# Two causal convolutions moved from channels in partitions to tokens in partitions, in a two-layer hybrid transformer kernel

## The chip, the cores and the metric

The kernel runs on one core of one Trainium2 chip. The metric is the device time of one execution in microseconds (us). Three runs of the kernel before took 2628.22, 2629.81 and 2631.31 us; their median, 2629.81 us, is the time before.

## What is computed

The reference takes 256 tokens of 2048 features through two layers. Each layer is a normalization, one wide input projection, several mixers on slices of the projection, output projections and a feed-forward part. Two of the mixers are preceded by a causal convolution of width 4 over the tokens, one filter per channel, then `silu`:

```python
def causal_dwconv(u, w, bias):          # layer 1, state space inputs, 1536 channels
    out = lax.conv_general_dilated(u, w[:, None, :], (1,), ((SSD_CONV - 1, 0),), ...)
    return out + bias
xbc = jax.nn.silu(causal_dwconv(xbc, conv_w, conv_b))
xs, bm, cm = _split(xbc, (SSD_WIDTH, N_BC, N_BC))      # 1024 + 256 + 256 channels
...
qkv = jax.nn.silu(causal_depthwise_conv(qkv, conv_w))  # layer 2, delta rule, 3072 channels
q, k, v = jnp.split(qkv, 3, axis=-1)                   # 1024 channels each
...
vb = v * beta[..., None]
```

So a channel's output at token i is `w[3]·u[i] + w[2]·u[i-1] + w[1]·u[i-2] + w[0]·u[i-3]`, plus the bias in layer 1, through `silu(y) = y·sigmoid(y)`. The kernel writes that as `h·(tanh(h) + 1)` with `h = y/2`, which is why its taps and biases are halved. In layer 1 the `xs` part is multiplied by the step sizes and by the skip weights, with tokens in partitions; in layer 2 `v` is multiplied by `beta`, with tokens in partitions too.

## The kernel before

The Tile framework schedules the program: it orders each engine's instructions when the program is built, by readiness in its own model of time and by the order in which they are written, picks the slots of each pool and sets all semaphores. On the chip each engine then runs its own list in that fixed order.

**Panels.** Nearly all of TensorE's work is projections. `panel` computes 256 tokens by up to 512 columns over 16 blocks of the contraction. Every 4 blocks it loads a weight tile `wst` on SP's queue (L201, pool of 3), and for each half of that tile ScalarE makes `whi`, the weights rounded to fp32r (L207, pool of 4), and VectorE makes `wlo`, the rest (L208, pool of 4). Each pair `whi`, `wlo` then feeds 12 matmuls of 512 columns: three products (L192 to L194) for two contraction blocks and two halves of the tokens. All other work of the mixers is laid between these matmuls.

**The convolutions.** `conv_group` (L692) takes the two PSUM tiles of a panel (tokens in partitions, 512 channels). ScalarE scales them into `raw` (L696); TensorE transposes `raw` in eight 128x128 blocks, so that channels lie in partitions (L703); ScalarE multiplies by the last tap (L708 with bias, L710 without); VectorE adds the other three taps with shifted reads along the free dimension, three instructions for each of four channel blocks (L713); then `tanh` (L715) and the product (L716). It is called nine times: for three panels of the state space inputs (L731 to L746: p = 0 and 1 are `xs`, p = 2 is `bm` and `cm`) and for six panels of the delta rule (`gdn_in`, L924: parts k, q, v for two groups of four heads). Where the consumer wants tokens in partitions, `to_tokens` (L719) transposes back, four blocks for each half of the tokens: for `xs` (L741, with ScalarE's copy at L742, then VectorE's products L743 and L744), for the sums of squares of k and q in `gdn_in`, and for `v` in each of the four calls of `gdn_unit` (L990, then the product with `beta` at L991).

**Order around the change.** State space inputs follow the sparse attention of layer 1 and precede the two z panels. In layer 2 the written order is `gdn_in(0)`, `gdn_unit(0, 0)`, `gdn_in(1)`, `gdn_unit(0, 1)`, `gdn_unit(1, 0)`, `gdn_unit(1, 1)`, two more z panels, then the other attention's panels; a unit's long chain of small products runs while panels written later fill TensorE.

**Pools.** `sp` has 7 slots and `s4` 17, of 4 KB per partition each; `s2` has 16 of 2 KB. Before, a convolution holds one `sp` tile (`raw`) and two `s4` tiles (`acc`, `th`). POOL (GpSimd) issues no DMA in this kernel; it computes powers in `rstd` (L159) and clears small tiles (L1004). SP's queue carries the weight tiles; ScalarE's queue carries small loads.

Of the kernel before, what the change touches and what calls it, by code (L numbers as in the profile page):

```python
# [12 lines left out]
AF = mybir.ActivationFunctionType  # L13
# [44 lines left out]
def build(ctx, tc, I, out, tap=None, upto=99):  # L58
# [22 lines left out]
    def s2(shape, dt=F32, name="s2"):  # L81
        return sb.tile(shape, dt, name=name, tag="s2", bufs=N2)
# [4 lines left out]
    def tiny(shape, name, bufs=2):  # L87
        return sm.tile(shape, F32, name=name, bufs=bufs)
# [603 lines left out]
    def conv_group(ps, r, taps, bias):  # L692

        raw = sp([128, 2, 512], name="raw")
        for t in range(2):
            S.activation(raw[:, t], ps[t], AF.Copy, scale=r[:, t:t + 1])  # L696
        acc = s4([128, 4, 256], name="acc")
        for j in range(0, 4, 2):
            pt = psum("tp", [128, 512])
            pv = pt.rearrange("p (k t c) -> p k t c", k=2, t=2)  # L700
            for kk in range(2):
                for t in range(2):
                    PE.transpose(pv[:, kk, t], raw[:, t, (j + kk) * 128:(j + kk + 1) * 128], ident)  # L703
            for kk in range(2):
                c = j + kk
                u = pt[:, kk * 256:(kk + 1) * 256]
                if bias is not None:
                    S.activation(acc[:, c], u, AF.Identity, scale=taps(3, c), bias=bias(c))  # L708
                else:
                    S.activation(acc[:, c], u, AF.Copy, scale=taps(3, c))  # L710
                for k in (2, 1, 0):
                    d = 3 - k
                    V.scalar_tensor_tensor(acc[:, c, d:], u[:, :256 - d], taps(k, c), acc[:, c, d:], op0=OP.mult, op1=OP.add)  # L713
        th = s4([128, 4, 256], name="th")
        S.activation(th, acc, AF.Tanh)  # L715
        V.scalar_tensor_tensor(acc, th, 1.0, acc, op0=OP.add, op1=OP.mult)  # L716
        return acc

    def to_tokens(src, t):  # L719

        ps = psum("tp", [128, 512])
        for c in range(4):
            PE.transpose(ps[:, c * 128:(c + 1) * 128], src[:, c, t * 128:(t + 1) * 128], ident)
        return ps

    def v8(ap):
        return ap.rearrange("p (h d) -> p h d", d=64)

    xsd, xdt = [], []
    BC = None  # L730
    for p in range(3):  # L731
        ps = panel(w_in, 0, 16, 1024 + 512 * p, 512, at_k(xn))
        xc = conv_group(ps, r, lambda j, c: conv_w[:, j * 12 + 4 * p + c:j * 12 + 4 * p + c + 1],
                        lambda c: conv_b[:, 4 * p + c:4 * p + c + 1])
        tap(f"xc{p}", xc)
        if p < 2:
            xsd.append(s4([128, 2, 512], name="xsd"))
            xdt.append(s4([128, 2, 512], name="xdt"))
            for t in range(2):
                pt = to_tokens(xc, t)  # L740
                xs = s2([128, 512], name="xs")  # L741
                S.activation(xs, pt, AF.Copy)  # L742
                V.tensor_tensor(v8(xsd[p][:, t]), v8(xs), b3(d_skip[:, 8 * p:8 * p + 8], 64), op=OP.mult)  # L743
                V.tensor_tensor(v8(xdt[p][:, t]), v8(xs), b3(dts[:, t, 8 * p:8 * p + 8], 64), op=OP.mult)  # L744
        else:
            BC = xc  # L746
# [47 lines left out]
        V.scalar_tensor_tensor(dst, dst, 1.0, ps[t][:, :n], op0=OP.add, op1=OP.mult)  # L794

    yssd = []
    rh = tiny([128, 2], "rh")
    V.tensor_scalar(rh, r, 0.5, None, op0=OP.mult)
    for g in range(2):
        ps = panel(w_in, 0, 16, 512 * g, 512, at_k(xn))  # L800
        ssg = tiny([128, 2], "ssg")
# [122 lines left out]
    def gdn_in(gi):  # L924
        qkv = [None] * 3
        kr, rks, rqs = [], [], []
        for part in (1, 0, 2):
            c0 = 2584 + part * 1024 + gi * 512
            ps = panel(w_in2, 0, 16, c0, 512, at_k(xn))
            if gi == 0 and part == 1:  # L930
                decays()
            ch = part * 8 + gi * 4
            qkv[part] = conv_group(ps, r, lambda j, c: P3[:, j * 24 + ch + c:j * 24 + ch + c + 1], None)
            if part == 2:
                continue
            for t in range(2):
                pt = to_tokens(qkv[part], t)
                sq = s2([128, 4, 128], name="gsq")
                S.activation(flat(sq), pt, AF.Square)
                ss = tiny([128, 4], "sg")  # L940
                V.tensor_reduce(ss, sq, axis=AX.X, op=OP.add)
                if part == 1:
                    kr.append(s2([128, 4, 128], name="kr"))
                    S.activation(flat(kr[t]), pt, AF.Copy)
                    rks.append(rstd(ss, 1.0, f"rk{t}"))
                else:
                    rqs.append(rstd(ss, 1.0, f"rq{t}", 128 ** -0.5))
        GD[gi] = qkv, kr, rks, rqs

    def gdn_unit(gi, t):  # L950
# [33 lines left out]
        for dst, rhs in ((A, lambda i: kbT[:, i]), (W, lambda i: qkv[0][:, i, ts])):  # L984
# [1 line left out]
            for i in range(4):  # L986
                PE.matmul(ps[:, i * 128:(i + 1) * 128], qkv[1][:, i, ts], rhs(i), start=True, stop=True)
            V.tensor_tensor(flat(dst), ps, flat(D), op=OP.mult)
        pt = to_tokens(qkv[2], t)
        vb = s2([128, 4, 128], name="vb")  # L990
        V.tensor_tensor(vb, hd(pt), b3(beta[:, t, hs], 128), op=OP.mult)  # L991

        Tt = s2([128, 4, 128], name="Tt")
        V.tensor_tensor(Tt, A, mid(lv[:, 0:128], 4), op=OP.mult)
# [454 lines left out]
```

## Time and profile before

| | |
|---|---|
| median of three runs | 2629.81 us (2628.22 to 2631.31) |
| the profiled execution | 2627.55 us, of which the span of instructions is 2625.8 us |
| TensorE (PE) busy | 2595.6 us, 99% of the span |
| VectorE (DVE) busy | 2136.2 us, 81% |
| ScalarE (ACT) busy | 1495.5 us, 57% |
| GpSimd (POOL) busy | 43.3 us, 2% |
| DMA | 478.65 MB, mean 182 GB/s |
| granted TensorE clock | 0.997 of full speed over the run |

PE stands for TensorE's matmuls and PEld for its weight loads, which overlap them. A matmul's end is modelled in the profile, so the time that one costs is read from start to start of neighbours and not from its duration. L12 is line 12 of the kernel. "mm" is a panel's PSUM tile, "tp" one for transposes, "sx" one for small products.

### The profile page before, as it was taken

What the parts mean: (1) busy time and instruction counts of PE and PEld (TensorE: products, weight loads), DVE (VectorE), ACT (ScalarE), POOL (GpSimd) and SP (SyncE); (2) the same over time, 40 slices, a digit from 0 to 9 for tenths busy, and PEclk for the clock granted to TensorE, in tenths of its full rate; (3) what the DMA queues carried; (4) which work ended last, traced back from release to release, by engine and by line L of the source; (5) the groups of instructions that cost most, each with busy time, mean ns of one, the idle gap of its engine ahead of it and who ended that gap; (6) DMA issues with size and microseconds to landing.
All of it is one profiled execution on the core that took longest, in us unless ns stands there. A gap on an engine that the chain in (4) does not pass through costs nothing.

```text
span 2625.8 us, 32837 instructions
## 1 busy us (share of the span) xinstructions
PE 2595.6 (99%) x12521; PEld 2164.9 (82%) x12521; DVE 2136.2 (81%) x2970; ACT 1495.5 (57%) x2002; POOL 43.3 (2%) x48
## 2 busy tenths in 40 slices
PE   8999999999999999999999999999999999999998
PEld 8998887888888888888898887888778888888886
DVE  5767789999989999676755867588999999999996
ACT  5455456656657566554533655455667566565663
POOL 0000000000000000000000000000000000000000
PEclk9999999999999999999999999999999999999999
DMA  7454555566655655753432843556455555565554
GB/s 239 143 177 156 169 178 186 183 204 199 196 202 192 194 193 194 227 184 126 132 98 87 263 166 115 178 193 224 170 197 181 206 193 208 192 206 191 196 192 161
DMA packets 181916, 478.65 MB, mean 182 GB/s; under 512 B 9127, under 2 KB 50046, under 8 KB 181758
## 3 DMA queue, kind: packets, MB, share of 16 engines
q1 hardware_dynamic: 175312, 467.05, 53.3%
q10 hardware_dynamic: 6446, 9.51, 1.1%
q8 instruction: 98, 1.61, 0.2%
q14 instruction: 60, 0.49, 0.1%
HBM read 472.32 MB, written 4.21 MB: 181 GB/s over the span
## 4 chain that ended last, share of the span: by engine, by line
PE 88%; DVE 7%; DMA 2%; ACT 2%; issue 1%; ACTq 0%; POOL 0%; POOLq 0%; SPq 0%; DVEq 0%
PE mm L270 24%; PE tp L270 12%; PE sx L270 11%; PE mm L194 10%; PE mm L192 10%; PE mm L193 10%; DVE wlo L282 3%; DMA wst<-in_w_down_dram 1%; ACT whi L281 1%; PE sx L1022 1%; PE sx L1017 1%; PE mm L430 1%; DVE t L303 1%; DMA wst<-in_w_in_dram 1%; PE tp L916 0%
## 5 line engine op out<-in xcount | busy, mean ns | idle before, releaser
L281 ACT ACTIVATE whi<-wst 128x1024 fp32r<-128x1024 f32 (+1 forms) x560 | 543.2, 980 | 312.8 <-PE mm L270 123.7
L282 DVE TENSOR_TENSOR wlo<-wst,whi 128x1024 fp32r<-128x1024 f32 (+1 forms) x560 | 615.8, 1120 | 67.2 <-ACT whi L281 65.1
L208 DVE TENSOR_TENSOR wlo<-wst,whi 128x1024 fp32r<-128x1024 f32 (+6 forms) x336 | 377.4, 1128 | 207.2 <-ACT whi L207 205.6
L207 ACT ACTIVATE whi<-wst 128x1024 fp32r<-128x1024 f32 (+6 forms) x336 | 329.5, 983 | 323.2 <-PE mm L194 290.3
L281 ACT ACTIVATE whi<-t 128x1024 fp32r<-128x1024 f32 x210 | 222.3, 1058 | 260.4 <-DVE t L307 118.7
L282 DVE TENSOR_TENSOR wlo<-t,whi 128x1024 fp32r<-128x1024 f32 x210 | 256.3, 1222 | 49.4 <-ACT whi L281 46.7
L194 PE MATMUL mm<-whi,x2l 128*128 128x512 f32 (+3 forms) x608 | 229.7, 378 | 0.0
L193 PE MATMUL mm<-wlo,x2h 128*128 128x512 f32 (+3 forms) x608 | 228.2, 375 | 1.4 <-DVE wlo L208 1.4
L192 PE MATMUL mm<-whi,x2h 128*128 128x512 f32 (+3 forms) x608 | 228.4, 376 | 0.0
L192 PE MATMUL mm<-whi,xnh 128*128 128x512 f32 (+3 forms) x416 | 152.5, 368 | 2.0 <-ACT whi L207 1.6
L270 PE MATMUL mm<-wlo,xnh 128*128 128x512 f32 x392 | 153.6, 392 | 0.5 <-DVE wlo L282 0.3
L270 PE MATMUL mm<-whi,xnl 128*128 128x512 f32 x392 | 153.1, 390 | 0.0
L270 PE MATMUL mm<-whi,xnh 128*128 128x512 f32 x392 | 151.3, 391 | 1.3 <-ACT whi L281 1.3
L193 PE MATMUL mm<-wlo,xnh 128*128 128x512 f32 (+3 forms) x416 | 151.8, 365 | 0.0
L194 PE MATMUL mm<-whi,xnl 128*128 128x512 f32 (+3 forms) x416 | 150.7, 365 | 0.0
L303 DVE TENSOR_TENSOR t<-wst 128x1024 f32<-128x1024 f32 x105 | 128.2, 1221 | 13.9 <-DMA wst<-in_w_down_dram 10.5
L270 PE MATMUL mm<-wlo,hTh 128*128 128x512 f32 x343 | 134.3, 391 | 0.6 <-DVE wlo L282 0.6
L270 PE MATMUL mm<-whi,hTl 128*128 128x512 f32 x343 | 133.6, 389 | 0.0
L270 PE MATMUL mm<-whi,hTh 128*128 128x512 f32 x343 | 132.1, 391 | 0.0
L193 PEld LDWEIGHTS mm<-wlo,x2h 128*128 128x128 f32 x608 | 114.7, 189 | 17.1 <-DVE wlo L208 2.0
L194 PEld LDWEIGHTS mm<-whi,x2l 128*128 128x128 f32 x608 | 114.5, 188 | 15.4 <-issue 1.0
L192 PEld LDWEIGHTS mm<-whi,x2h 128*128 128x128 f32 x608 | 114.7, 189 | 15.0 <-issue 0.8
(619 smaller groups left out, 5697.2 us busy)
## 6 DMA issues: line engine op xcount, KB each, us to landing
wst<-in_w_up_dram SPq DMA_DIRECT2D x128, 1024.0 KB, 5.1
wst<-in_w_down_dram SPq DMA_DIRECT2D x128, 1024.0 KB, 5.5
wst<-in_w_in_dram SPq DMA_DIRECT2D x84, 1024.0 KB, 5.0
wst<-in_w_out_dram SPq DMA_DIRECT2D x16, 1024.0 KB, 5.5
wst<-in_w_o_dram SPq DMA_DIRECT2D x16, 1024.0 KB, 5.2
wst<-in_w_in_dram SPq DMA_DIRECT2D x16, 780.0 KB, 4.5
wst<-in_w_in_dram SPq DMA_DIRECT2D x12, 824.0 KB, 4.5
wst<-in_w_in_dram SPq DMA_DIRECT2D x12, 736.0 KB, 6.9
```

Of the source, the lines that this page charges most:

```text
L192: PE.matmul(ps[t][:, :n], xh[:, sl], wa, start=kt == first, stop=False)
L193: PE.matmul(ps[t][:, :n], xh[:, sl], wb, start=False, stop=False)
L194: PE.matmul(ps[t][:, :n], xl[:, sl], wa, start=False, stop=kt == last)
L207: S.activation(a[:, :2 * n], src, AF.Copy)
L208: V.tensor_tensor(b[:, :2 * n], src, a[:, :2 * n].bitcast(F32), op=OP.subtract)
L270: PE.matmul(B[b], x, y, start=left[b] == total[b], stop=left[b] == 1)
L281: S.activation(a[:, :n], src, AF.Copy)
L282: V.tensor_tensor(b[:, :n], src, a[:, :n].bitcast(F32), op=OP.subtract)
L303: V.tensor_tensor(t13, s.rearrange("p (k l n) -> p k l n", k=2, l=2)[:, :, 0], s[:, :1024].rearrange("p (l n) -> p l n", l=2)[:, ::-1], op ...
L430: PE.transpose(pv[:, kk, t, :], us[t, l][:, c:c + 128], ident)
L1017: PE.matmul(ps[:, i * 64:(i + 1) * 64].rearrange("p (m b) -> p m b", b=b), N[:, i], half(T[:, i], 0), start=True, stop=True)
L1022: PE.matmul(ps[:, i * 64:(i + 1) * 64].rearrange("p (m b) -> p m b", b=b), P[:, i], half(Tt[:, i], 1), start=True, stop=True)
```

## The change

A new function `conv_tokens` convolves with tokens in partitions. ScalarE scales the panel's PSUM into `raw` (now with half the normalization factor, `rh`, moved up for that). The four taps of the 512 channels come as rows, broadcast to all partitions by two DMAs of 512 KB on SP's queue (`tb`). For each shift d = 1, 2, 3 GpSimd issues two DMAs from SBUF to SBUF: rows 0 to 127-d of both token halves to rows d to 127, and the last d rows of the first half to the first d rows of the second; VectorE clears the first d rows of the first half. VectorE multiplies `raw` and the three shifted copies by their tap rows and adds them up, on tiles of 128x1024. `tanh` and the last product are as before, on the other layout; `th` moves from the `s4` pool to `sp`.

It is used in four of the nine places: p = 0 and 1 of the state space inputs (with a bias row, loaded by a DMA of 256 KB on SP's queue and halved by ScalarE) and part v of both groups of the delta rule. There `raw` isn't transposed, `to_tokens` isn't called, and the copy `xs` falls away; the other five convolutions stay as they were.

```diff
+    def conv_tokens(ps, rh, name, c0, bias=None):
+        w = I[name][0] if len(I[name].shape) == 3 else I[name]
+        wd = w.shape[1]
+        raw = sp([128, 2, 512], name="raw")
+        for t in range(2):
+            S.activation(raw[:, t], ps[t], AF.Copy, scale=rh[:, t:t + 1])
+        tb = [s4([128, 2, 512], name="tb") for _ in range(2)]
+        for q in range(2):
+            nc.sync.dma_start(tb[q], bass.AP(tensor=w.tensor, offset=w.offset + 2 * q * wd + c0,
+                                             ap=[[0, 128], [wd, 2], [1, 512]]))
+        acc = s4([128, 2, 512], name="acc")
+        def row(j):
+            return mid(tb[j // 2][:, j % 2], 2)
+        V.tensor_tensor(acc, raw, row(3), op=OP.mult)
+        if bias is not None:
+            V.tensor_tensor(acc, acc, mid(bias, 2), op=OP.add)
+        for d in (1, 2, 3):
+            sh = sp([128, 2, 512], name="sh")
+            V.memset(sh[:d, 0], 0.0)
+            G.dma_start(sh[d:], raw[:128 - d])
+            G.dma_start(sh[:d, 1], raw[128 - d:, 0])
+            V.tensor_tensor(sh, sh, row(3 - d), op=OP.mult)
+            V.tensor_tensor(acc, acc, sh, op=OP.add)
+        th = sp([128, 2, 512], name="th")
+        S.activation(th, acc, AF.Tanh)
+        V.scalar_tensor_tensor(acc, th, 1.0, acc, op0=OP.add, op1=OP.mult)
+        return acc
...
+    rh = tiny([128, 2], "rh")
+    V.tensor_scalar(rh, r, 0.5, None, op0=OP.mult)
...
-        xc = conv_group(ps, r, lambda j, c: conv_w[:, j * 12 + 4 * p + c:j * 12 + 4 * p + c + 1],
-                        lambda c: conv_b[:, 4 * p + c:4 * p + c + 1])
+        if p < 2:
+            bb = s2([128, 512], name="bb")
+            cb_ = I["conv_b"]
+            nc.sync.dma_start(bb, bass.AP(tensor=cb_.tensor, offset=cb_.offset + 512 * p, ap=[[0, 128], [1, 512]]))
+            S.activation(bb, bb, AF.Copy, scale=0.5)
+            xc = conv_tokens(ps, rh, "conv_w", 512 * p, bb)
+        else:
+            xc = conv_group(ps, r, lambda j, c: conv_w[:, j * 12 + 4 * p + c:j * 12 + 4 * p + c + 1],
+                            lambda c: conv_b[:, 4 * p + c:4 * p + c + 1])
...
-                pt = to_tokens(xc, t)
-                xs = s2([128, 512], name="xs")
-                S.activation(xs, pt, AF.Copy)
+                xs = xc[:, t]
...
+            if part == 2:
+                qkv[part] = conv_tokens(ps, rh, "conv_w_2", ch * 128)
+                continue
...
-        pt = to_tokens(qkv[2], t)
         vb = s2([128, 4, 128], name="vb")
-        V.tensor_tensor(vb, hd(pt), b3(beta[:, t, hs], 128), op=OP.mult)
+        V.tensor_tensor(vb, hd(qkv[2][:, t]), b3(beta[:, t, hs], 128), op=OP.mult)
```

## Rows read from the trace of the kernel before

**Rows 1.** The page: engines (busy us, share of the span, instructions).

```profile
PE 2595.6 (99%) x12521; PEld 2164.9 (82%) x12521; DVE 2136.2 (81%) x2970; ACT 1495.5 (57%) x2002; POOL 43.3 (2%) x48
```

**Rows 2.** The page, chain that ended last: shares of the span by engine.

```profile
PE 88%; DVE 7%; DMA 2%; ACT 2%; issue 1%; ACTq 0%; POOL 0%; POOLq 0%; SPq 0%; DVEq 0%
```

**Rows 3.** Busy time by stretch: length, PE, PEld, DVE, ACT, POOL, clock, DMA share, GB/s.

```profile
206.00:231.00 25.00, 25.00 (x122) 20.66 (x121) 18.91 (x30) 14.78 (x19) 0.00 (x0) 1.00 0.42 130
231.00:255.00 24.00, 24.00 (x115) 19.63 (x114) 18.10 (x26) 13.73 (x17) 0.00 (x0) 1.00 0.55 176
...
1189.00:1213.00 24.00, 24.00 (x126) 20.24 (x126) 21.40 (x37) 12.07 (x17) 0.53 (x1) 1.00 0.48 159
...
1284.00:1308.00 24.00, 24.00 (x164) 23.52 (x162) 22.30 (x42) 13.58 (x22) 0.79 (x2) 1.00 0.41 121
```

**Rows 4.** One line each: transposes there (L703) and back (L723), ns min/median/max.

```profile
L703 PE MATMUL tp<-idt,raw x72: 270/273/328, 208.6 to 1285.1; 128*128 128x128 f32 x72
...
L723 PE MATMUL tp<-idt,acc x64: 270/273/303, 221.7 to 1397.4; 128*128 128x128 f32 x64
```

**Rows 5.** Timeline of PE around the eight transposes back (start, us, instruction).

```profile
221.46 0.39 PE L194 MATMUL mm<-whi,xnl 128*128 128x512 f32 x1
221.69 1.03 PE L723 MATMUL tp<-idt,acc 128*128 128x128 f32 x8
222.48 0.48 PE L192 MATMUL mm<-whi,xnh 128*128 128x512 f32 x1
222.80 0.40 PE L193 MATMUL mm<-wlo,xnh 128*128 128x512 f32 x1
```

**Rows 6.** Timeline of PE around the eight transposes there, p = 1.

```profile
232.13 0.39 PE L192 MATMUL mm<-whi,xnh 128*128 128x512 f32 x1
232.39 0.44 PE L703 MATMUL tp<-idt,raw 128*128 128x128 f32 x2
...
233.14 0.82 PE L703 MATMUL tp<-idt,raw 128*128 128x128 f32 x6
...
234.03 0.40 PE L193 MATMUL mm<-wlo,xnh 128*128 128x512 f32 x1
```

**Rows 7.** Timeline of DVE in the convolution of p = 1.

```profile
235.14 2.42 DVE L713 SCALAR_TENSOR_TENSOR acc<-tp,P2T,acc 128x255 f32<-128x255 f32 x6
237.48 1.22 DVE L208 TENSOR_TENSOR wlo<-wst,whi 128x1024 fp32r<-128x1024 f32 x1
...
243.82 1.22 DVE L716 SCALAR_TENSOR_TENSOR acc<-th,acc 128x1024 f32<-128x1024 f32 x1
```

**Rows 8.** Groups of DVE by form: its two clears (count, busy us, mean ns).

```profile
L1137 DVE MEMSET flu<- 128x64 f32 x4 | 0.4, 112 | 0.0
L1265 DVE MEMSET Pc<- 128x120 f32 x2 | 0.3, 158 | 0.0
```

**Rows 9.** Timeline of ACT: two `whi` of p = 1's panel.

```profile
226.89 1.06 ACT L207 ACTIVATE whi<-wst 128x1024 fp32r<-128x1024 f32 x1 [1.67 <-PE mm L194]
229.61 1.06 ACT L207 ACTIVATE whi<-wst 128x1024 fp32r<-128x1024 f32 x1 [1.66 <-PE mm L194]
```

**Rows 10.** DMA: one queue (packets, MB, share of 16 engines), then issues to landing.

```profile
q1 hardware_dynamic: 175312, 467.05, 53.3%
...
wst<-in_w_in_dram SPq DMA_DIRECT2D x84, 1024.0 KB, 5.0
...
X<-in_x_dram SPq DMA_DIRECT2D x4, 512.0 KB, 8.6
X<-in_x_dram ACTq DMA_DIRECT2D x4, 512.0 KB, 4.8
...
lnf<-in_ln_f_w_dram ACTq DMA_DIRECT2D x4, 256.0 KB, 6.0
```

**Rows 11.** Timeline of POOL around gdn_in(0).

```profile
1158.02 1.01 POOL L159 TENSOR_TENSOR rk<-rv,mhalf 128x4 f32<-128x4 f32 x1 [0.43 <-DVE rv L157]
...
1183.12 1.91 POOL L159 TENSOR_TENSOR rq<-rv,mhalf 128x4 f32<-128x4 f32 x1 [0.35 <-DVE rv L157]
```

More of the change, by code (lines that the diff above doesn't have):

```diff
@@ L796, in build @@
     yssd = []
-    rh = tiny([128, 2], "rh")
-    V.tensor_scalar(rh, r, 0.5, None, op0=OP.mult)
     for g in range(2):
@@ L932, in gdn_in @@
             ch = part * 8 + gi * 4
+            if part == 2:
+                qkv[part] = conv_tokens(ps, rh, "conv_w_2", ch * 128)
+                continue
             qkv[part] = conv_group(ps, r, lambda j, c: P3[:, j * 24 + ch + c:j * 24 + ch + c + 1], None)
-            if part == 2:
-                continue
             for t in range(2):
```

## The prediction

> **What bounds the kernel.** I read the page first: TensorE is busy 99% of the span, VectorE 81%, ScalarE 57%, POOL 2% [rows 1]. The chain that ended last says the same of the path to the end: 88% of it is PE [rows 2]. An average hides stages, so I then took the busy times of the four stretches in which the four convolutions that change are worked off [rows 3]: in each, PE is busy from its first to its last microsecond at the full clock, while VectorE has 2 to 6 us left of 24 or 25. So a microsecond of TensorE's own work that goes is a microsecond of the kernel, as long as the weight halves `wlo` still come in time; work taken from ScalarE or given to POOL is worth nothing by itself.
>
> How much time `wlo` has is read from ScalarE's timeline [rows 9]. Each `whi` starts when a matmul lets go of one of the four slots, every 2.72 us (226.89 to 229.61). At that moment three pairs, 3 x 2.72 = 8.16 us of matmuls, still lie ready. `whi` takes 1.06 us and `wlo` 1.22 [rows 7, 9], so a `wlo` made at once is there 8.16 - 2.28 = 5.9 us before it is wanted. These 5.9 us are the cover for all that VectorE does first, or waits for first.
>
> **What goes from TensorE.** Eight transposes back cost this: the matmul at 221.46 and its neighbour at 221.69 show the usual step of 0.23 us; without the transposes the second matmul after 221.46 would start 0.46 later, and it starts at 222.80, 1.34 later, so 0.88 us for eight [rows 5]. Eight transposes there: between 232.13 and 234.03 lie four steps of matmuls, 0.91 us, of 1.90 in all, so 0.99 us, the switches to and fro among them [rows 6]. The 72 and 64 transposes of the two lines [rows 4] are nine and eight groups of eight. The change takes four of the nine groups there (4 x 0.99 = 4.0 us). Of those back it takes p = 0 and 1 (2 x 0.88 = 1.8) and the four units' (4 x 4 transposes, two more groups, 1.8; split in four they may cost a little more). Together 7.6, with the finer splitting 7.7 us, 0.29% of the run. Nothing is added on TensorE.
>
> **What VectorE gets.** Before, a convolution costs it twelve shifted multiply-adds, six in 2.42 us, and the last product of 1.22: 6.1 us [rows 7]. After, it has eight instructions on 128x1024 with both inputs in SBUF (one product, three times product and sum, the last product), nine with the bias, each priced as `wlo`, which has that shape: 9.8 or 11.0 us. The three clears have no row of their size; the two of 64 and 120 columns took 112 and 158 ns [rows 8], 0.82 ns per column, so 0.48 us for 512, an estimate, 1.4 for three (nothing, if they fit into idle time: their tiles are free early). So a `v` convolution gains up to 5.1 us and an `xs` one up to 6.4. Laid on the stretches, which lose 1.0 or 1.9 us of TensorE work: 25.3 us of VectorE's work for 23.1, 24.5 for 22.1, 26.5 for 23.0, 27.4 for 23.0 [rows 3]. It is 2.2 to 4.4 us too much in each, 12.5 in all.
>
> Not all of that is lost, as it is drawn from the 5.9 us first and the stretches between have room. What decides is the order: the convolution is written before the next panel, so it goes first where both are ready. If product and sum of all three shifts follow one another, a `wlo` stands behind six instructions, 6 x 1.22 = 7.3 us, 1.4 more than its cover; a `wlo` that gets between them, as one did between the two sixes at 237.48 [rows 7], loses nothing. **Bounds of what is given back:** from 0 (a `wlo` between each pair, clears hidden) to 4 x 1.4 + 12.5 = 18.1 us (the excess finds no cover). I take 1.4 for each convolution, 5.6 us: the three copies pass through the same queue close together, which favours the row of six, while the excess has until the next stretch to be made up.
>
> **The copies and loads.** POOL issues 24 DMAs, six for a convolution, three of them of 500 to 508 KB. No row shows a DMA of its queue. The nearest are the loads of 512 KB on the other queues, which land 4.8 or 8.6 us after issue [rows 10]; a copy that waits for nothing but itself could take less. Six issues would sit on a queue that is idle nearly throughout [rows 1], where a small power takes 1.01 or 1.91 us for the same form [rows 11]. What is behind the waiting copies there are the powers and clears of the units, which come later. The wait that counts is VectorE's: the product with a shifted copy waits for it, and behind that stand the `wlo` of the next panel in a fixed order. I cost it at nothing, with the 5.9 us as cover, and price its loss under the rivals.
>
> SP's queue gets eight tap loads of 512 KB and two bias loads of 256 KB ahead of weight tiles. 467.05 MB took 53.3% of the 16 engines, so they move 334 GB/s when busy. One `xs` convolution adds 1.5 MB of copies and 1.3 MB of loads in 22 us, 128 GB/s on top of 130 and 176 [rows 3, 10]: up to 304 of 334. The loads ahead of a weight tile delay it by 1.3 MB at 334 GB/s, 3.9 us. A tile lands 5.0 us after issue, and its slot came free when two more tiles, 10.9 us, were still to be split: 5.9 us of cover again. So nothing, but little is left; a tap load that waited for a slot of `s4` for over 2 us would cost what goes beyond.
>
> ScalarE loses the tap products and the copy `xs` and gains two halvings of the bias; it is under 60% busy there [rows 3]. `xsd`, `xdt` and `vb` keep their instructions and read SBUF instead.
>
> **Sum.** -7.7 + 5.6 = -2.1 us. The profiled execution took 2627.55 us, its span 2625.8 and 1.75 around it, so its sum is 2625.4; the median of the three runs is 2.3 us above that execution, which makes 2627.7. About 0.2%, 5.3 us, is what a measurement of this kernel can tell from no change.
>
> **Rivals.**
> - **Forecast: the gain is mostly given back (0.40).** 2627.7; with 2.4 to 13 us given back, 2624.5 to 2635, within 0.2%.
> - **The cover holds (0.27).** `wlo` comes between the pairs and nothing is late: 2629.8 - 7.7 = 2622.1, faster. For it: the `wlo` at 237.48, which came between two blocks of a convolution unharmed [rows 7]. Against it: the excess just worked out.
> - **The copies come late and VectorE stands (0.26).** VectorE's order is fixed when the program is built. If it counts on a copy after 4.8 us and gets it after 8.6 [rows 10], VectorE stands 3.8 us in front of ready weight halves, four times; with the 7.3 us after it that is 5.2 beyond the cover each: -7.7 + 20.8 gives 2642.9, slower. It decides once wait and row of six together pass 5.9 us by 3.2 in each convolution (12.9 us in all). For it: DMA load up to 304 of 334 GB/s, and a POOL that needs up to twice as long beside VectorE [rows 11]. Against it: a first copy that is late also lets the third come no later, so the six instructions are then no row.
> - **One DMA engine carries the copy of 127 rows (0.07).** 508 KB at 334 / 16 = 20.9 GB/s take 25 us; VectorE stands 20 us longer than with 4.8, 21.5 beyond the cover with the row of six, four times: -7.7 + 86 gives 2708. The Trainium skill (DMA: Bandwidth & Descriptors, "Why a DMA increments its semaphore by 16 and not by 1") states the rule for it: a DMA is split over the largest number up to 16 that divides its slowest dimension, 1 for 127. The same section reports an exception on trn2, by which some direct copies from GpSimd run 127 rows on all 16; no row before shows either, and for the exception I leave the case 7 in 100.
>
> The Trainium skill (same page, "Anatomy of one DMA") prices a GpSimd copy at 2.0 us plus its bytes at 436 GB/s, an estimate of 3.2 us for 508 KB; by that no copy is late and the sum is the forecast's or the 2622.1 above it. The load rows of 4.8 and 8.6 us stand against so short a time.
>
> **Numbers.** 2627.7 is the likeliest case; its own range is 2624.5 to 2635. The range for 8 in 10 goes from 2620, below the full saving by the scatter of the runs, to 2650, which holds the late copies up to nearly 7 us each and leaves out the single engine and the worst of the late. Faster 0.27, same 0.40, slower 0.26 + 0.07 = 0.33.
>
> **What would show it.** L703 at 40 and L723 at 32 transposes; PE's busy time 7 to 8 us lower whatever the span does. In PE's waits: `wlo` rows (L208) of about a microsecond after each of the four convolutions mean the forecast; none, the cover; several of 3 us or more, and VectorE waiting for a DMA into `sh`, late copies. The copies' time to landing near 25 us for 127 rows and far less for 126 and 125 would mean the single engine. Waits of ScalarE for `wst` in these stretches would mean that the loads on SP's queue cost after all. I am wrong altogether if the time changes where none of the four convolutions lies, since Tile orders the whole program anew.

## The result and the profile after

The changed kernel takes 2653.21 us (median of five runs, 2652.28 to 2656.70), the kernel before, run beside it, 2628.22 (median of five): ratio 1.0096, 95% interval 1.0085 to 1.0107, 25 us slower. The prediction said 2627.7, 2620 to 2650. The profiled execution took 2656.70 us, its span 2654.8.

In the changed kernel the copies are L740 and L741, the products with the shifted copies L742, their sums L743, the product with the unshifted values L734, the bias L736, the clears L739 and the last product L746. The page's engines and its chain by engine:

```profile
PE 2597.4 (98%) x12457; PEld 2164.7 (82%) x12457; DVE 2156.7 (81%) x2964; ACT 1487.2 (56%) x1984; POOL 56.9 (2%) x72
...
PE 83%; DVE 9%; DMA 4%; ACT 2%; issue 1%; POOL 0%; ACTq 0%; POOLq 0%; SPq 0%; DVEq 0%
```

64 matmuls fewer, the transposes that went, yet PE's busy time is 1.8 us longer than in [rows 1], and the chain gives 9% to VectorE and 4% to DMA instead of 7% and 2% [rows 2]. The stretches of [rows 3], same columns (length, PE, PEld, DVE, ACT, POOL, clock, DMA share, GB/s):

```profile
206.00:231.00 25.00, 23.07 (x104) 18.69 (x103) 22.80 (x27) 12.71 (x17) 3.32 (x6) 1.00 0.74 217
231.00:255.00 24.00, 15.93 (x65) 12.81 (x64) 17.25 (x18) 8.01 (x9) 3.11 (x6) 0.88 0.75 218
1189.00:1213.00 24.00, 21.38 (x108) 17.54 (x106) 17.67 (x27) 10.43 (x13) 7.48 (x10) 1.00 0.66 193
1284.00:1308.00 24.00, 24.00 (x127) 20.79 (x126) 18.15 (x33) 10.87 (x15) 6.81 (x9) 1.00 0.61 186
```

PE had no gap in them before; now 1.9 of 25 us are missing in the first, 8.1 of 24 in the second and 2.6 in the third, and VectorE, which was to be fuller, is emptier in the second and third: it waits. (The fourth convolution lies later than before; PE's stop for it comes at 1313.) What PE waits for (line waited for: us in total, times, longest), first in 195 to 330 us, the state space inputs, then in 1120 to 1480, the delta rule:

```profile
PE mm L193 <- DVE wlo L208: 10.0, 2, 8.1
...
PE mm L193 <- DVE wlo L208: 9.3, 3, 5.5
PE sx L1023 <- ACT qgT L1013: 4.4, 2, 2.6
```

And what VectorE waits for in the same two stretches (one row of each):

```profile
DVE sh L742 <- DMA sh<-raw: 8.6, 4, 5.1
...
DVE sh L742 <- DMA sh<-raw: 5.7, 3, 2.6
```

VectorE's timeline in the convolution of p = 1 shows how the one becomes the other:

```profile
236.33 1.21 DVE L734 TENSOR_TENSOR acc<-raw,tb 128x1024 f32<-128x1024 f32 x1
242.63 1.23 DVE L742 TENSOR_TENSOR sh<-sh,tb 128x1024 f32<-128x1024 f32 x1 [5.10 <-DMA sh<-raw]
243.78 1.22 DVE L736 TENSOR_TENSOR acc<-acc,bb 128x1024 f32<-128x1024 f32 x1
245.83 1.22 DVE L742 TENSOR_TENSOR sh<-sh,tb 128x1024 f32<-128x1024 f32 x1 [0.84 <-DMA sh<-raw]
246.97 1.22 DVE L743 TENSOR_TENSOR acc<-acc,sh 128x1024 f32<-128x1024 f32 x1
248.85 1.23 DVE L742 TENSOR_TENSOR sh<-sh,tb 128x1024 f32<-128x1024 f32 x1 [0.66 <-DMA sh<-raw]
250.00 1.22 DVE L743 TENSOR_TENSOR acc<-acc,sh 128x1024 f32<-128x1024 f32 x1
251.13 1.22 DVE L208 TENSOR_TENSOR wlo<-wst,whi 128x1024 fp32r<-128x1024 f32 x1
```

The `wlo` at 251.13 follows the one that ended at 236.40, 14.7 us earlier. Both engines make the halves in the same order, so its `whi` is this one of ScalarE's timeline, ready at 236.82:

```profile
235.76 1.06 ACT L207 ACTIVATE whi<-wst 128x1024 fp32r<-128x1024 f32 x1 [1.08 <-PE mm L194]
```

For 14.3 us nothing but VectorE's order kept it waiting: it stood behind a product that waited for a copy, and then behind the rest of the row, with two more waits in it. PE's timeline says what that cost:

```profile
243.72 0.61 PE L192 MATMUL mm<-whi,xnh 128*128 128x512 f32 x2
252.40 0.79 PE L193 MATMUL mm<-wlo,xnh 128*128 128x512 f32 x1 [8.07 <-DVE wlo L208]
252.99 0.63 PE L194 MATMUL mm<-whi,xnl 128*128 128x512 f32 x1
253.42 0.63 PE L193 MATMUL mm<-wlo,xnh 128*128 128x512 f32 x1
```

It stops for 8.07 us and starts again with steps of 0.43 us, not 0.23. The granted clock by windows (columns as above) tells why: it is 0.50, that is 1.2 of 2.4 GHz, until 256. The first window, in the stop, has the DMA engines full (share 1.02) while the copies land.

```profile
244.00:248.00 4.00, 0.34 (x2) 0.00 (x0) 3.16 (x3) 0.98 (x1) 0.00 (x0) 1.00 1.02 271
...
254.00:256.00 2.00, 2.00 (x7) 1.52 (x6) 2.00 (x3) 0.57 (x1) 0.00 (x0) 0.50 0.27 24
256.00:258.00 2.00, 2.00 (x10) 1.66 (x9) 2.00 (x3) 1.06 (x1) 0.00 (x0) 0.95 0.85 294
```

Nine steps, from 252.40 to 256.32, took 3.92 us; at 0.227 they take 2.04. So 1.9 us go to the restart.

**Where the 25 us lie.** The lines L192 to L194 and L270 do the projections' matmuls, 10437 of them in every trace of this study. I compared the start of the same count in two traces: no. 840 (197 us) lies ahead of the state space inputs, no. 1320 (334 us) behind them, no. 4920 (1183 us) ahead of the delta rule, no. 5940 (1506 us) behind it. After against before: state space stage +8.5 us, between the two +3.2, delta-rule stage +14.3, behind it +2.6. The two stages make 22.8 of the 29.0 us by which these two traces differ (the medians differ by 25.0). A part of the rest is the clock: it is 0.50 from 431 to 437 and from 1574 to 1580, longer than at the same places before (423 to 426, 1549.5 to 1552), by my estimate from the steps of 0.43 and 0.23 us about 1.6 us in each. That the change causes this is not shown.

In the delta rule too the clock fell after PE's stops:

```profile
1219.00:1222.00 3.00, 3.00 (x9) 2.32 (x8) 3.00 (x6) 0.00 (x0) 0.00 (x0) 0.50 0.78 229
1318.00:1324.00 6.00, 5.00 (x16) 4.55 (x17) 6.00 (x9) 0.79 (x1) 0.00 (x0) 0.50 0.40 118
```

### The profile page after: what moved, and what is told of

It reads as the page before. It is cut to its first block, busy times and chain, and to the rows that moved or that the text cites. A ratio compares the mean times of both kernels' runs of the same rounds, so it can differ in the third digit from the quotient of the medians.

```text
span 2654.8 us, 32753 instructions
## 1 busy us (share of the span) xinstructions
PE 2597.4 (98%) x12457; PEld 2164.7 (82%) x12457; DVE 2156.7 (81%) x2964; ACT 1487.2 (56%) x1984; POOL 56.9 (2%) x72
## 4 chain that ended last, share of the span: by engine, by line
PE 83%; DVE 9%; DMA 4%; ACT 2%; issue 1%; POOL 0%; ACTq 0%; POOLq 0%; SPq 0%; DVEq 0%
PE mm L270 22%; PE tp L270 12%; PE sx L270 11%; PE mm L193 10%; PE mm L194 10%; PE mm L192 10%; DVE wlo L282 4%; DMA wst<-in_w_down_dram 2%; DMA sh<-raw 1%; ACT whi L281 1%; PE sx L1057 1%; PE sx L1052 1%; DVE t L303 1%; PE mm L430 1%; DVE wlo L208 0%
## 5 line engine op out<-in xcount | busy, mean ns | idle before, releaser
L282 DVE TENSOR_TENSOR wlo<-wst,whi 128x1024 fp32r<-128x1024 f32 (+1 forms) x560 | 615.6, 1120 | 67.9 <-ACT whi L281 65.3
L194 PE MATMUL mm<-whi,x2l 128*128 128x512 f32 (+3 forms) x608 | 232.2, 382 | 0.0
L192 PE MATMUL mm<-whi,x2h 128*128 128x512 f32 (+3 forms) x608 | 229.3, 379 | 0.0
L192 PE MATMUL mm<-whi,xnh 128*128 128x512 f32 (+3 forms) x416 | 152.5, 369 | 2.0 <-ACT whi L207 1.6
L270 PE MATMUL mm<-wlo,xnh 128*128 128x512 f32 x392 | 153.5, 392 | 0.3 <-DVE wlo L282 0.3
L270 PE MATMUL mm<-whi,xnl 128*128 128x512 f32 x392 | 153.1, 391 | 0.0
L270 PE MATMUL mm<-whi,xnh 128*128 128x512 f32 x392 | 151.3, 391 | 1.3 <-ACT whi L281 1.3
L194 PE MATMUL mm<-whi,xnl 128*128 128x512 f32 (+3 forms) x416 | 151.6, 367 | 0.1
L270 PE MATMUL mm<-wlo,hTh 128*128 128x512 f32 x343 | 134.3, 391 | 1.2 <-DVE wlo L282 1.2
L270 PE MATMUL mm<-whi,hTl 128*128 128x512 f32 x343 | 133.6, 390 | 0.0
L270 PE MATMUL mm<-whi,hTh 128*128 128x512 f32 x343 | 131.9, 390 | 0.0
L192 PEld LDWEIGHTS mm<-whi,x2h 128*128 128x128 f32 x608 | 115.7, 190 | 15.7 <-issue 1.4
L194 PEld LDWEIGHTS mm<-whi,x2l 128*128 128x128 f32 x608 | 116.0, 191 | 15.1 <-issue 0.9
```

The costliest lines, as they stand in the source:

```text
L192: PE.matmul(ps[t][:, :n], xh[:, sl], wa, start=kt == first, stop=False)
L194: PE.matmul(ps[t][:, :n], xl[:, sl], wa, start=False, stop=kt == last)
L270: PE.matmul(B[b], x, y, start=left[b] == total[b], stop=left[b] == 1)
L282: V.tensor_tensor(b[:, :n], src, a[:, :n].bitcast(F32), op=OP.subtract)
```

## The experiments

**Theory A:** VectorE's list is fixed when the program is built; in it the products stand ahead of `wlo`, and on the chip the copies land later than this order needs. **Theory B:** the longer convolution delays `wlo` by its work alone, above all in the delta rule. **Theory C:** the traffic of the copies delays the weight tiles. The ratios are to the kernel before, run beside each on the same chip (medians 2628.54 us for the first four runs; 2625.55 for xs alone with products later, the two on the work of v, and the first with v spread; 2626.40 for xs alone as changed and the last three). Times that were expected for those of the second and third group start from 2628.5 and so lie 2 to 3 us too high for the chip of the run; I compare ratios there. A stage's figure is its length by matmul counts less that in the trace of before.

**No copies.** The products read `raw` unshifted; clears and copies are left out.

```diff
-            V.memset(sh[:d, 0], 0.0)
-            G.dma_start(sh[d:], raw[:128 - d])
-            G.dma_start(sh[:d, 1], raw[128 - d:, 0])
-            V.tensor_tensor(sh, sh, row(3 - d), op=OP.mult)
+            V.tensor_tensor(sh, raw, row(3 - d), op=OP.mult)
```

> Leaves the shifted copies out: the four products all read raw, so the convolution adds four taps of the same token; VectorE keeps its eight or nine large instructions for each convolution, and the tap loads stay. Theory A (VectorE stands before the copies and the weight halves behind it come late): 2618 to 2628 us, TensorE waits for wlo less than 5 us in all. Theory B (VectorE's added work alone starves TensorE): 2640 us or more, with several us of waits for wlo at each of the four places. Theory C (the traffic of copies delays the weight tiles): as A, with no wait for wst.

2637.13 us, ratio 1.0032 (1.0021 to 1.0044), between A's 2618 to 2628 and B's 2640 or more: each holds in one stage. The state space stage is 2.6 us shorter than before, most of what its transposes cost: there the copies were the whole loss. The delta-rule stage is still 6.3 us longer. VectorE's timeline there:

```profile
1286.81 0.69 DVE L997 COPY kbT<-tp 128x512 f32<-128x512 f32 x1 [1.46 <-PE tp L948]
1287.42 1.22 DVE L734 TENSOR_TENSOR acc<-raw,tb 128x1024 f32<-128x1024 f32 x1
1288.55 2.35 DVE L739 TENSOR_TENSOR sh<-raw,tb 128x1024 f32<-128x1024 f32 x2
...
1298.92 1.13 DVE L1014 SCALAR_TENSOR_TENSOR D<-D,rk,C 128x128 f32<-128x128 f32 x4
1299.97 0.88 DVE L208 TENSOR_TENSOR wlo<-wst,whi 128x696 fp32r<-128x696 f32 x1
```

13.2 us of work without a pause and without a `wlo`: the eight instructions of the convolution and those of the unit's chain (`kbT`, `kbg`, `D`, `qgT`) take turns. PE's waits name both things that came late, 1120 to 1480 us:

```profile
PE sx L1020 <- ACT qgT L1010: 5.2, 2, 3.5
PE mm L193 <- DVE wlo L208: 2.3, 2, 1.3
```

**Copies that nobody reads.** As above, but clears and copies run and land.

```diff
             G.dma_start(sh[:d, 1], raw[128 - d:, 0])
-            V.tensor_tensor(sh, sh, row(3 - d), op=OP.mult)
-            V.tensor_tensor(acc, acc, sh, op=OP.add)
+            V.tensor_tensor(pr, raw, row(3 - d), op=OP.mult)
+            V.tensor_tensor(acc, acc, pr, op=OP.add)
```

> Leaves the use of the shifted copies out: they are issued and land as in the changed kernel, but the products read raw, so nothing waits for a copy. Theory A: 2618 to 2630 us, as without copies. Theory B: 2640 us or more. Theory C (traffic): 2640 us or more, with ScalarE waiting for wst in the four stretches, where the run without copies does not.

2635.49 us, 1.0027 (1.0017 to 1.0037): no slower than without copies, and in the two stages the same, -2.7 and +6.4. ScalarE does wait 3.9 us once for a weight tile in the state space stage, where the run without copies waits for none, but PE stops no longer there than in that run (0.5 us in all, 0.7 without copies). Theory C falls as a cause of the loss.

**Copies on ScalarE's queue**, the long ones in two pieces (112 rows and the rest).

```diff
-            G.dma_start(sh[d:], raw[:128 - d])
-            G.dma_start(sh[:d, 1], raw[128 - d:, 0])
+            S.dma_start(sh[d:112 + d], raw[:112])
+            S.dma_start(sh[112 + d:], raw[112:128 - d])
+            S.dma_start(sh[:d, 1], raw[128 - d:, 0])
```

> The copies go out on ScalarE's queue, 112 rows in one DMA and the rest in another, so nine DMAs for a convolution. If GpSimd's queue is what makes them late: they land in 3 to 5 us, VectorE waits under 4 us for them, 2625 to 2640 us. If the DMA engines are full at that time: landing stays at 5 to 13 us and the time at 2645 to 2660 us.

2654.88 us, 1.0095 (1.0080 to 1.0110), as slow as the changed kernel: the time is the one expected for full DMA engines. But VectorE's waits for copies are shorter in the state space stage (2.5 us in all instead of 8.6; 5.2 instead of 5.7 in the delta rule), and something else has come in. ScalarE stands while it issues the copies, at p = 1 nine of them from 233.6 to 240.8, ahead of four `whi`:

```profile
240.85 3.90 ACT L207 ACTIVATE whi<-wst 128x1024 fp32r<-128x1024 f32 x4 [5.97 <-DMA sh<-raw]
```

So PE still waits, 4.5 us at the longest in that stage (+6.9) and 9.0 in the delta rule (+18.1). The run shows that a change of queue alone doesn't help; whether POOL's queue makes the copies late stays open.

**Products later.** The same work; products, tanh and last product are a function of their own, called for xs after the next panel is written, for v in the unit that needs it, ahead of `vb`.

```diff
+        def rest():
+            for d, sh in zip((1, 2, 3), shs):
+                V.tensor_tensor(sh, sh, row(3 - d), op=OP.mult)
...
+        return rest
...
+        if pend is not None:
+            xs_rest(p - 1, pend())
...
+        if t == 0:
+            qkv[2] = qkv[2]()
         vb = s2([128, 4, 128], name="vb")
```

> Same instructions and copies; the products with the shifted copies, tanh and last product are written later: after the next panel for the state space inputs, in the first unit for the delta rule's values. Theory A: copies have long landed, VectorE never stands for them, 2618 to 2628 us and so faster than the kernel before by the 7.7 us of transposes less up to 5. Theory B: the same work still comes in a row before some panel's weight halves, 2640 us or more. Theory C: the traffic is the same, 2640 us or more.

2637.31 us, 1.0033 (1.0020 to 1.0046), between the two expectations again. The state space stage is 3.7 us shorter than before, just what the transposes were priced at, and PE waits for nothing there. VectorE's timeline at p = 1 now:

```profile
238.95 1.22 DVE L208 TENSOR_TENSOR wlo<-wst,whi 128x1024 fp32r<-128x1024 f32 x1
240.09 1.22 DVE L736 TENSOR_TENSOR acc<-acc,bb 128x1024 f32<-128x1024 f32 x1
241.22 1.22 DVE L747 TENSOR_TENSOR sh<-sh,tb 128x1024 f32<-128x1024 f32 x1
242.36 1.22 DVE L208 TENSOR_TENSOR wlo<-wst,whi 128x1024 fp32r<-128x1024 f32 x1
243.49 1.22 DVE L748 TENSOR_TENSOR acc<-acc,sh 128x1024 f32<-128x1024 f32 x1
244.63 1.22 DVE L208 TENSOR_TENSOR wlo<-wst,whi 128x1024 fp32r<-128x1024 f32 x1
```

Written behind the panel, the products fill in between the `wlo`, and by then the copies have landed. In the delta rule the same step failed (+11.7 us): the products are pulled forward all the same, into an earlier unit's chain, ahead of their copies (a wait of 2.47 us at 1290) and then among the chain's own steps, and PE waits 6.3 us for one of these (`Tt`). That the scheduler does so because VectorE counts as free while the chain waits for PE is my reading, not shown.

**The xs half alone, products later** (v as before).

```diff
-            if part == 2:
-                qkv[part] = conv_tokens(ps, rh, "conv_w_2", ch * 128)
-                continue
             qkv[part] = conv_group(ps, r, lambda j, c: P3[:, j * 24 + ch + c:j * 24 + ch + c + 1], None)
+            if part == 2:
+                continue
...
+        pt = to_tokens(qkv[2], t)
         vb = s2([128, 4, 128], name="vb")
-        V.tensor_tensor(vb, hd(qkv[2][:, t]), b3(beta[:, t, hs], 128), op=OP.mult)
+        V.tensor_tensor(vb, hd(pt), b3(beta[:, t, hs], 128), op=OP.mult)
```

> The xs half of the change alone, with products, sums, tanh and last product of each xs convolution written after the next panel; v as before (transposed there and back). Sixteen groups' worth of saving becomes eight: 3.7 us. Theory A (the state space stage loses only because VectorE stands in front of late copies): 2628.5 - 3.7 = 2624.8 us, 2623.5 to 2626. Rival (the new order of the whole program costs something wherever it falls): 2628 to 2634, with the state space stage still 3.7 faster by itself.

(The groups of eight transposes that go are eight in the whole change and four here, not sixteen and eight; the 3.7 us are right.) 2626.43 us, 1.0003 (0.9994 to 1.0011): a miss for the whole time. The state space stage is 3.5 us shorter as expected, but the interval excludes a whole gain of 3.7 us. As a ratio it would suit the rival (0.9998 to 1.0021), but the new order isn't there: outside the stage the order of PE, VectorE and ScalarE is that of before. I come back to it under the last run.

**The xs half alone, as changed**: the changed kernel with the same edit of v, products right behind the copies.

> The xs half of the change as it is in the changed kernel, products right behind the copies, and v as before. Theory A (VectorE stands for the copies, weight halves late): before + 8 to 10 us, ratio 1.0030 to 1.0038, of which the changed kernel's 25 us takes its first third; the wait of PE for wlo near 250 us of the run is 8 us again. Rival (the state space stage was hit only together with the later one, by an order that this kernel doesn't have): ratio 0.998 to 1.001.

2641.22 us, 1.0058 (1.0044 to 1.0071), above the expected band; its state space stage is +9.0 (the whole change's: +8.5), with PE waiting 8.8 us for `wlo`, 6.6 at the longest. Theory A holds for that stage by itself; the other 3.5 us of its trace lie elsewhere.

**The work of v, by amount.** xs later; v in tokens, its products reading unshifted values as in the first run: three of them, or one (the products and sums of the other two taps left out). The cut shows the run with three.

```diff
+        if raws:
+            for d in raws:
+                sh = sp([128, 2, 512], name="sh")
+                V.tensor_tensor(sh, raw, row(3 - d), op=OP.mult)
+                V.tensor_tensor(acc, acc, sh, op=OP.add)
...
-                qkv[part] = conv_tokens(ps, rh, "conv_w_2", ch * 128)
+                qkv[part] = conv_tokens(ps, rh, "conv_w_2", ch * 128, raws=(1, 2, 3))
```

> The xs half as in the run above; v in tokens too, but its copies and clears are left out: the three products read the unshifted values (another result, the same eight VectorE instructions, no DMA between them). Theory A (only standing in front of copies costs): 2628.5 - 7.7 = 2620.8. Theory B (in the delta-rule stage the 9.8 us of VectorE's work in one row cost by themselves, 6 to 12 us): 2624.8 + 6 to 12, so 2631 to 2637.

> As the run with three products that read unshifted values, but with one of them: products and sums of two taps are left out, so a v convolution has four VectorE instructions on 128x1024, 4.9 us, under the 6.1 of before. Theory B: the loss goes with the work, so 2620.8 to 2623, 8 to 14 us under the run with three. Rival (what costs is the order in which v's convolution falls among the unit's steps, not how much it is): 2630 to 2636, within 3 us of the run with three.

With three: 2634.34 us, 1.0031 (1.0019 to 1.0043), delta-rule stage +7.5; so B. With one: 2624.83, 0.9997 (0.9988 to 1.0006), stage -1.7: 9.5 us under the run with three, as B expected, but not the 5.5 to 7.7 us under the kernel before that B meant. The loss shrinks with the work by 9.2 us but doesn't go. The run with one product still has such a row:

```profile
1278.21 0.88 DVE L208 TENSOR_TENSOR wlo<-wst,whi 128x696 fp32r<-128x696 f32 x1 [1.22 <-ACT whi L207]
1280.55 0.69 DVE L1016 COPY kbT<-tp 128x512 f32<-128x512 f32 x1 [1.46 <-PE tp L967]
...
1288.15 1.13 DVE L1033 SCALAR_TENSOR_TENSOR D<-D,rk,C 128x128 f32<-128x128 f32 x4
1289.20 0.87 DVE L208 TENSOR_TENSOR wlo<-wst,whi 128x696 fp32r<-128x696 f32 x1
```

8.7 us from `kbT` to the next `wlo`, though the convolution is only 4.9 of them. Amount alone can't decide, then; the order had to be tried.

**v spread.** The whole change with its copies. xs later; v's product and sum of shift 1, 2, 3 behind the first three levels of the unit's triangular inversion, the last product behind the fourth, each tied behind that level's instruction on VectorE so that it can't be pulled forward.

```diff
-            V.tensor_tensor(halves(Tt, 1), halves(Tt, 1), packed(ps), op=OP.subtract)
+            ins = V.tensor_tensor(halves(Tt, 1), halves(Tt, 1), packed(ps), op=OP.subtract)
+            if t == 0 and l < 5:
+                with tc.issue_after(ins.ins):
+                    if l < 4:
+                        qkv[2][0](l)
+                    else:
+                        qkv[2] = qkv[2][1]()
```

> The whole change with its copies, computing the same as the reference: xs as in the first of these runs, and v's product and sum of one shift put behind each of the first three levels of the triangular inversion that needs vb last, the last product behind the fourth. Theory B in its form of a row (a weight half stands behind six instructions in a row; in pairs it doesn't): the full saving but for a little, 2621 to 2625. B in its form of a total (VectorE has no time left in this stage, wherever the work is put): 2631 to 2637. Theory A alone: as the first form, since the copies have landed long before.

2621.20 us, 0.9981 (0.9972 to 0.9990), faster than both kernels: 4.4 us of the 7.7 that the transposes were priced at. All the VectorE work is there, more than the run with three unshifted products had, and the delta-rule stage is 6.8 us shorter than before. So what cost was the row and the waits in it, not the total. (The same edit writes the product with `beta`, `vb`, behind the inversion; that move wasn't tried by itself.)

**v spread alone; the whole once more; and before's order.** xs as before in the first (the cut is against the changed kernel); the second repeats the run above; the third is the kernel before, with only `rh` written earlier.

```diff
-            xc = conv_tokens(ps, rh, "conv_w", 512 * p, bb)
+        xc = conv_group(ps, r, lambda j, c: conv_w[:, j * 12 + 4 * p + c:j * 12 + 4 * p + c + 1],
+                        lambda c: conv_b[:, 4 * p + c:4 * p + c + 1])
```

> The v half of the run with v's pairs spread over the inversion, alone: xs as before the change, transposed there and back. That run's trace passed the delta-rule stage 6.8 us faster than the kernel before, 2.9 more than the 3.9 us of transposes that v saves. If that holds by itself: before less 3.9 to 6.8 us, ratio 0.9974 to 0.9985. If most of what a stage saves is lost again in the stages behind it (the run with xs alone kept nothing of 3.7 us): within 0.2% of before, ratio 0.9990 to 1.0005.

> The kernel with xs written later and v spread, once more, beside v spread alone and beside before's order on one chip. If the two savings add up: v spread alone less 3.7 us, ratio near 0.9960. If xs keeps nothing, as it did alone: within 1 us of v spread alone. In the first run its ratio was 0.9981; in either case the interval should hold that or meet it.

```diff
+    rh = tiny([128, 2], "rh")
+    V.tensor_scalar(rh, r, 0.5, None, op0=OP.mult)
     xsd, xdt = [], []
...
     yssd = []
-    rh = tiny([128, 2], "rh")
-    V.tensor_scalar(rh, r, 0.5, None, op0=OP.mult)
```

> The kernel before with nothing changed but the place where rh, a 128x2 product, is written (which the change moves ahead of the convolutions); every engine's order stays as it was. Any theory: ratio 0.9995 to 1.0005. It gives a trace of before's order on the chip of these runs; where it differs by over 1 us from the trace of before in some stage, such a difference between traces is the chip's and not a kernel's.

v alone: 2622.75 us, 0.9988 (0.9979 to 0.9996), stage -6.8. The whole: 2620.76, 0.9977 (0.9968 to 0.9986), stages -3.8 and -6.7. Neither met its expectations squarely: v alone lies between keeping its saving and losing it, with an interval that meets both, and the whole is 2.0 us under v alone, not 3.7 and not within 1. VectorE's timeline of that run in the second convolution's stretch:

```profile
1280.71 0.87 DVE L208 TENSOR_TENSOR wlo<-wst,whi 128x696 fp32r<-128x696 f32 x1
...
1283.15 0.87 DVE L208 TENSOR_TENSOR wlo<-wst,whi 128x696 fp32r<-128x696 f32 x1
...
1285.74 0.87 DVE L208 TENSOR_TENSOR wlo<-wst,whi 128x696 fp32r<-128x696 f32 x1
```

A `wlo` every 2.5 us where the runs above had none for 8.7 to 13.2. Its windows, by the columns of [rows 3], have PE full again in the two stretches that had suffered most:

```profile
231.00:255.00 24.00, 23.99 (x110) 19.66 (x109) 22.79 (x24) 11.65 (x13) 2.93 (x6) 1.00 0.91 275
1189.00:1213.00 24.00, 24.00 (x142) 20.27 (x142) 20.52 (x28) 9.78 (x14) 1.58 (x3) 1.00 0.60 183
```

Its two stages save 10.5 us, its time 5.6. Before's order with `rh` moved: ratio 1.0002 (0.9993 to 1.0011), so moving `rh` costs nothing; but its trace differs from that of before, with the same orders on PE, VectorE and ScalarE, by 2.5 us behind the delta rule. Between executions of the same order the stages behind differ that much, and in the spread runs these stages took up to 2.4 us more than in the trace of before, 3.7 to 4.9 more than in this one. A part of it is the clock: the trace of before has stretches at 0.50 at 423, 1550 and 2574, the one with `rh` moved only at 1549, and each is worth about 1.6 us by the same estimate. Whether a saved stage makes the later ones slower, which would also explain the run of xs alone, isn't settled: a comparison of single traces can't tell it from this scatter.

## Why the prediction was wrong

**What went from TensorE** was right for xs: 3.7 us predicted, 3.5 to 3.8 measured in the stage. For v 3.9 were predicted and 6.7 to 6.8 measured with v spread; about 1 us is PE's waits of before that went with it, and where the rest comes from stays open. L703 has 40 transposes, L753 (L723 before) 32, as said:

```profile
L703 PE MATMUL tp<-idt,raw x40: 270/273/328, 265.0 to 1279.9; 128*128 128x128 f32 x40
...
L753 PE MATMUL tp<-idt,acc x32: 270/273/299, 1166.5 to 1292.2; 128*128 128x128 f32 x32
```

That PE's busy time would be 7 to 8 us lower "whatever the span does" was wrong: at half clock a matmul is busy for longer (0.63 instead of 0.39 us at p = 1). In the second run of the whole with v spread, where PE waits for nothing in either stage, it is 10.0 us lower (2585.6).

**What VectorE gets** was right: 20.5 us more busy [rows 1] where the terms make up to 23.

**The step that failed** is "I cost it at nothing, with the 5.9 us as cover": VectorE's wait for the copies. It stood 14.3 us in front of them in all. DMA issues to landing (KB each, median us):

```profile
tb<-in_conv_w_dram SPq DMA_DIRECT2D x8, 512.0 KB, 7.0
...
sh<-raw POOLq DMA_DIRECT2D x4, 508.0 KB, 5.2
sh<-raw POOLq DMA_DIRECT2D x4, 504.0 KB, 7.7
sh<-raw POOLq DMA_DIRECT2D x4, 500.0 KB, 8.4
```

Those are the bounds that I had read, 4.8 and 8.6 us [rows 10]; I priced the wait as if the lower one held, and for the second and third copy the upper was nearer. The Trainium skill's price (DMA: Bandwidth & Descriptors, "Anatomy of one DMA"), by which I had estimated 3.2 us, fits none of the three medians.

The give-back of 1.4 us for a convolution came out at 12.2 for the two xs (8.5 longer instead of 3.7 shorter: 10.0 of PE's waits, 8.1 of them at p = 1, and 1.9 of the restart), and at 18.2 for the two v (14.3 longer instead of 3.9 shorter: 13.7 of PE's waits and, by my estimate from the steps at 0.50, about 4 of the clock). Measured against the 6.8 us that v saves when spread it is 21.1.

**The late copies were the right rival, mis-sized:** 5.2 us each and 2642.9 in all. Four things were missing in it:

- "a first copy that is late also lets the third come no later, so the six instructions are then no row." At p = 1 six instructions (three products, the bias, two sums) stood ahead of the `wlo` all the same, with three waits among them (5.10, 0.84 and 0.66 us), since the order was fixed. Wait and row add up.
- After the long stop PE starts at half clock, 1.9 us more at p = 1. The trace of before had a row for this that the prediction doesn't use: after a stop of 2.59 us at 2571.6, for a tile of VectorE's, the clock falls too, and in the window below one matmul follows another after 0.43 us.

```profile
2574.00:2576.00 2.00, 2.00 (x6) 1.54 (x5) 0.97 (x2) 0.24 (x2) 0.00 (x0) 0.50 0.75 280
```

- The cover at the second v isn't 5.9 us. There panels of 348 columns are being multiplied: a step of 0.16 us and twelve steps for one `wlo` of 128x696 are 1.92 us, three pairs 5.8, less `whi` and `wlo` (0.79 and 0.88) 4.1 us. I had measured the cover in the state space stage and used it everywhere. (At the first v the panel still has 512 columns.)
- There the row isn't the convolution's alone. The unit's chain stands in it too, and PE waits for that as well (`qgT`, 4.4 us). "The `wlo` of the next panel" named one of the two things that are queued behind.

So without any copy the delta rule still lost (+6.3). The row was in the forecast's sum, at 1.4 us for a convolution, and was mis-sized there: 10.2 us for the two v even where no copy is waited for.

**One DMA engine for 127 rows** was wrong: 508 KB landed in 5.2 us at the median, and no copy took more than 12.8 us, against 25. The exception for GpSimd's direct copies that the Trainium skill reports (same page, "Why a DMA increments its semaphore by 16 and not by 1") is what the trace agrees with.

**The loads on SP's queue** cost nothing that can be told. The sign that I had named did come: ScalarE waits 1.9 us for `wst` at 241.4. But its `whi` lay ready long before VectorE reached it, and with products written later all the loads are there, PE waits for nothing in the state space stage, and that is 3.7 us shorter.

## What to carry to other kernels

Where an engine with a fixed order prepares operands for the bottleneck, look at the longest time between two such preparations, not at its busy share: here 14.7 us (with waits for copies) or 14.6 us (without, in the delta rule) against a cover of 4 to 6 us cost what the saved transposes brought and more, and with the same work in pairs between them PE didn't wait. A wait for a DMA in that order costs the wait and everything fixed behind it, so issue the copy, write its consumer one stage later, and tie it there if the scheduler would pull it forward. Measure the cover in each stage in which the change lands.

## What I had not expected of the hardware

After 8.07 us without a matmul TensorE ran the next nine steps at a granted clock of 0.50 (1.2 GHz), 3.92 us instead of 2.04; the stop cost a quarter more than its length. And two copies of 504 and 500 KB, issued about 1 us after one another behind the first, took 7.7 and 8.4 us to the first one's 5.2.
